# Feed-forward up-projections by Strassen's scheme: seven half-size products, weight sums on GpSimd, six chunks of middle features

## The chip, the cores and the metric

The kernel runs on one core of a Trainium2 chip. The metric is the device time of one launch in microseconds (us). The kernel before was run twice: 2931.71 and 2932.26 us, median 2931.99. The names of the engines are those of the profile: PE is TensorE (matmul), PEld its weight loads, DVE VectorE, ACT ScalarE, POOL GpSimd, SP SyncE, from whose queue most loads are issued.

## What is computed

Two trunk layers over 512 latent tokens and 256 context tokens of width 1024, all in float32. Each layer is a half-step feed-forward, a token mixer, and a second half-step feed-forward, each with its own modulation of shift, scale and gate from a condition vector. The second feed-forward of the last layer needs the latent tokens alone. Cut to what matters here:

```python
D_MODEL, SEQ, CTX_LEN, D_FF, DEPTH = 1024, 512, 256, 2816, 2

def swiglu(h, w_in, w_out):
    g, u = jnp.split(h @ w_in, 2, axis=-1)
    return (jax.nn.silu(g) * u) @ w_out

def half_ffn(x, m, name):
    sh, sc, g = m
    h = modulate(rms_norm(x, prm[name + "_norm"]), sh, sc)
    return x + 0.5 * g * swiglu(h, prm[name + "_w_in"], prm[name + "_w_out"])

xl = half_ffn(xl, mod_l[0:3], "ffn1")
xc = half_ffn(xc, mod_c[0:3], "ffn1")
...
ol, oc = mixer(hl, hc, prm, ctx_out, ropes)
xl = xl + mod_l[5] * ol
xl = half_ffn(xl, mod_l[6:9], "ffn2")
if ctx_out:
    xc = xc + mod_c[5] * oc
    xc = half_ffn(xc, mod_c[6:9], "ffn2")
```

## The kernel before, in words

Activations lie transposed: eight row tiles of 128 features by 768 tokens (512 latent, then 256 context). Float32 operands are split in two parts, a high part rounded to the format that PE multiplies quickly and a low part, the rest; a product of two split operands is three matmuls (high by high, high by low, low by high), written as `three` in `ffn`. Weights are split on the way: `unit` (L206) takes a raw block of 128 x 1024 that SP has loaded (`raw`, L201), ACT casts the high part (L210), and DVE subtracts for the low part (L211). There are two buffers for raw blocks and three sets of high and low parts.

`ffn` (L450) is called four times. The weight matrix of the up-projection comes in 44 units, in turn a gate unit and an up unit of 128 middle features. `product(u)` (L477) runs 8 row tiles x 3 terms x 2 token segments, 48 matmuls, into one of three pairs of PSUM banks: 512 and 258 columns, where 2 columns carry the shift; in the last feed-forward 256 and 258. `gate` (L510) multiplies both results by the token's rms factor (the norm is applied after the product), takes silu with the shift as bias on ACT, multiplies on DVE and splits the outcome. After each chunk of middle features (`CHUNKS`, 8, 7 and 7 tiles) `back` (L527) runs the down-projection of the chunk for each of 8 row tiles, and DVE adds it, times the modulation's gate, to the row tile (L538). After the last chunk `after` prepares the next stage: the sum of squares (`sq_acc`, L411: ACT squares, POOL adds) and the operand of the next feed-forward (`prep`, L422: POOL casts, DVE subtracts). Ahead of a mixer the last chunk is done in two parts, latent tokens first (`D0`, `split`), so that norm and mixer input start under the context's matmuls.

Beside it, `bg` (L385) advances the modulation of later stages by one step of `mod_dve` (L323): it loads 512 KB of weights and runs four multiply-adds of 512 columns on DVE (L338, L340); after four steps come two small groups of matmuls (L358, L367). It is called once per unit and once per row tile of a down-projection. 16 parts of 8 steps are done in this way.

The first feed-forward starts while x is still loading: `late` brings x into its operand within the first products, and the shift's columns follow as matmuls of their own (`shifts`, L502).

Which instruction comes when on an engine is set at build time by a scheduler: it takes what is ready in its own forecast of the run, in the order of the program. On the chip each engine then keeps that order, and waits on semaphores. SBUF beyond the weights is cut into twenty areas A0 to E3 (L153), which each tile takes over from the one before: x in A or D, operands in B and C, the split middle features in D or A (high) and E (low).

## Time and profile before

| what | value |
| --- | --- |
| runs | 2931.71 and 2932.26 us, median 2931.99 |
| span of the profiled execution, first to last instruction | 2929.3 us |
| its instructions | 41724 |
| matmuls, weight loads | 17276, 17276 |
| raw weight loads for each up-projection | 44 of 512 KB |
| loads of modulation weights | 140 of 512 KB |
| mean granted clock of PE | 0.982 |

The span is that of the one execution that was profiled; the median lies 2.7 us above it. A row of busy time by stage gives the stage's bounds and length in us, then for PE, weight loads, DVE, ACT and POOL the busy time with the number of instructions, and at the end the granted clock of PE, the share of the DMA engines' time and GB/s. A row of the timeline gives start, length, engine, line of the kernel, operation, what is written and read, its shape, and how many instructions were merged; in brackets stands idle time before it and what ended it. A row of the chain of waits gives start, length, and what the end of the program was waiting for at that time.

### The profile page before, as it was taken

Reading aid. Unit: us, or ns where it says so; the run is one execution under the profiler, and the core shown is the slowest. Engines: PE = TensorE matmul, PEld = TensorE weight load, DVE = VectorE, ACT = ScalarE, POOL = GpSimd, SP = SyncE. Lnnn points to the kernel's source line nnn. Section 1 sums busy time; section 2 is a strip of 40 time slices with the busy share of each in tenths; the row PEclk is TensorE's granted clock in tenths of the full one; section 3 lists DMA queues with packets and bytes.
Section 4 is the critical chain, followed back from the end, with each engine's and each line's share of the span. In section 5 each row is a group of like instructions: output and inputs, shape, how many; then the busy total and the mean of one; then the engine's idle time right before and its main releaser. Section 6 shows DMA issues by size and latency. Waiting matters only on the chain.

```text
span 2929.3 us, 41724 instructions
## 1 busy us (share of the span) xinstructions
PE 2812.6 (96%) x17276; PEld 2436.2 (83%) x17276; DVE 1708.6 (58%) x2709; ACT 855.1 (29%) x1281; POOL 460.0 (16%) x435
## 2 busy tenths in 40 slices
PE   8999999998479899999999999999999999999999
PEld 5888888887467788888888888888888888898998
DVE  2665666688987676656545533333336779643443
ACT  3211212242156522112122221121224257332221
POOL 1000000035943330000000300000011256300000
PEclk9999999999789999999999999999999999999999
DMA  6433343431010223333433111112124200222232
GB/s 219 129 122 124 120 139 116 127 124 46 31 42 2 72 87 120 118 116 116 140 126 102 59 63 66 59 60 69 59 86 126 65 12 30 87 94 94 88 97 90
DMA packets 93740, 266.62 MB, mean 91 GB/s; under 512 B 8816, under 2 KB 9968, under 8 KB 93552
## 3 DMA queue, kind: packets, MB, share of 16 engines
q1 hardware_dynamic: 86512, 247.89, 26.6%
q10 hardware_dynamic: 5376, 10.83, 1.2%
q0 software_dynamic: 1664, 5.24, 0.5%
q8 instruction: 136, 2.23, 0.3%
q14 instruction: 52, 0.43, 0.0%
HBM read 255.80 MB, written 7.34 MB: 90 GB/s over the span
## 4 chain that ended last, share of the span: by engine, by line
PE 88%; DVE 7%; ACT 2%; issue 1%; DMA 1%; POOL 1%; ACTq 0%; SPq 0%; DVEq 0%; POOLq 0%
PE pa L190 53%; PE pb L190 26%; DVE D L774 3%; PE p L706 2%; PE pb L659 2%; DVE wl L211 1%; PE pa L1035 1%; PE pa L1263 1%; PE p L358 1%; ACT t L661 1%; PE p L193 0%; DMA r<-in_modw 0%; DVE sm L672 0%; PE p L279 0%; DVE C L199 0%
## 5 line engine op out<-in xcount | busy, mean ns | idle before, releaser
L210 ACT CAST wh<-r 128x1024 fp32r<-128x1024 f32 (+3 forms) x334 | 340.6, 1020 | 1517.8 <-PE pa L190 776.1
L190 PE MATMUL pa<-B,wh 128*128 128x512 f32 (+1 forms) x1984 | 492.8, 330 | 10.9 <-DVE D L199 8.6
L190 PE MATMUL pa<-B,wl 128*128 128x512 f32 (+1 forms) x1984 | 487.5, 327 | 0.0
L190 PE MATMUL pa<-C,wh 128*128 128x512 f32 (+1 forms) x1984 | 487.0, 327 | 0.3 <-DVE C L428 0.3
L211 DVE TENSOR_TENSOR wl<-r,wh 128x1024 fp32r<-128x1024 f32 (+3 forms) x334 | 410.7, 1230 | 39.8 <-ACT wh L210 31.0
L190 PEld LDWEIGHTS pa<-B,wh 128*128 128x128 f32 x1984 | 308.6, 190 | 50.9 <-issue 15.8
L190 PEld LDWEIGHTS pa<-C,wh 128*128 128x128 f32 x1984 | 307.9, 190 | 35.7 <-issue 0.7
L190 PEld LDWEIGHTS pa<-B,wl 128*128 128x128 f32 x1984 | 307.7, 190 | 34.1 <-issue 0.5
L199 DVE SCALAR_TENSOR_TENSOR t<-m,sT,t 128x512 f32<-128x512 f32 x392 | 275.7, 752 | 3.9 <-DMA m<-in_modw 2.8
L190 PE MATMUL pa<-E,wh 128*128 128x512 f32 (+1 forms) x919 | 257.7, 347 | 1.3 <-POOL E L215 1.3
L517 DVE COPY sm<-pa 128x2 f32<-128x2 f32 x116 | 18.4, 159 | 395.7 <-PE pa L190 395.1
L190 PE MATMUL pb<-B,wh 128*128 128x512 f32 (+1 forms) x960 | 236.5, 328 | 0.0
L190 PE MATMUL pb<-B,wl 128*128 128x512 f32 (+1 forms) x960 | 234.0, 325 | 0.0
L190 PE MATMUL pb<-C,wh 128*128 128x512 f32 (+1 forms) x960 | 233.5, 324 | 0.0
L190 PE MATMUL pa<-D,wh 128*128 128x512 f32 (+1 forms) x777 | 204.4, 339 | 0.1
L190 PE MATMUL pa<-D,wl 128*128 128x256 f32 (+1 forms) x737 | 196.3, 339 | 0.0
L1416 POOL DMA_DIRECT2D xs<-A x24 | 13.5, 562 | 1089.0 <-DVE A L199 1087.3
L190 PEld LDWEIGHTS pa<-E,wh 128*128 128x128 f32 x919 | 148.2, 188 | 24.3 <-POOL E L215 1.7
L190 PEld LDWEIGHTS pb<-B,wh 128*128 128x128 f32 x960 | 148.6, 189 | 19.6 <-issue 4.2
L190 PEld LDWEIGHTS pb<-C,wh 128*128 128x128 f32 x960 | 148.2, 189 | 16.2
L190 PEld LDWEIGHTS pb<-B,wl 128*128 128x128 f32 x960 | 148.2, 189 | 15.8
L199 DVE SCALAR_TENSOR_TENSOR A<-pa,hg,A 128x256 f32<-128x256 f32 (+1 forms) x95 | 54.9, 614 | 172.1 <-PE pa L190 172.0
(329 smaller groups left out, 4470.3 us busy)
## 6 DMA issues: line engine op xcount, KB each, us to landing
m<-in_modw SPq DMA_DIRECT2D x140, 512.0 KB, 3.7
r<-in_win0a SPq DMA_DIRECT2D x44, 512.0 KB, 4.2
r<-in_win0b SPq DMA_DIRECT2D x44, 512.0 KB, 3.5
r<-in_win1a SPq DMA_DIRECT2D x44, 512.0 KB, 3.4
r<-in_win1b SPq DMA_DIRECT2D x44, 512.0 KB, 3.4
r<-in_wodd SPq DMA_DIRECT2D x18, 512.0 KB, 3.7
r<-in_wout0a SPq DMA_DIRECT2D x20, 448.0 KB, 3.5
r<-in_wout1a SPq DMA_DIRECT2D x20, 448.0 KB, 3.4
```

What stands on the lines that cost most here:

```text
L190: self.nc.tensor.matmul(out, l.bitcast(F32R), r.bitcast(F32R), start=st, stop=sp)
L199: self.nc.vector.scalar_tensor_tensor(o, a, s, b, op0=op0, op1=op1)
L210: pin(self.nc.scalar.copy(hi, r))
L211: pin(self.nc.vector.tensor_tensor(lo, r, hi.bitcast(F32), op=ALU.subtract))
L358: nc.tensor.matmul(p[g:g + 32, :], self.ones[:, 0:32], acc[v][:, q * 256:(q + 1) * 256], start=True, stop=True, tile_position=(0, g))
L517: nc.vector.tensor_copy(w2[:, o:o + 2], p[:, so:so + 2])
L659: pin(nc.tensor.transpose(pt[:, ks], P[:, ks], self.col("ident")))
L661: pin(nc.scalar.copy(PT[:, :m], pt[:, :m]))
L706: self.pin(self.nc.tensor.matmul(self.po[i * 64:(i + 1) * 64, col:col + 128], v, self.PTs[i][:, kt * 128:(kt + 1) * 128], start=(kt == 0), ...
L774: pin(nc.vector.scalar_tensor_tensor(cv, yw, dw[:, w:w + 1], cv, op0=ALU.mult, op1=ALU.add))
L1035: self.pin(nc.tensor.matmul(s[:, o:o + b - a], q[:, ts].bitcast(F32R), k[:, a:b].bitcast(F32R), start=j == 0, stop=j == 2))
L1263: self.pin(nc.tensor.matmul(s[:, a:b], q.bitcast(F32R), k[:, a:b].bitcast(F32R), start=j == 0, stop=j == 1))
```

## The change

The up-projection's product is cut in two along each of its three dimensions: the 1024 features in two halves of 4 row tiles, the output in gate and up, the tokens in two halves (each 256 latent and 128 context tokens, with 2 columns for the shift: 386; 258 in the last feed-forward). Eight half-size products become seven, by sums ahead of them and behind them.

- Weight sums: `group(j)` loads the gate unit R0 and the up unit R1. POOL forms S = R1a + R1b, R0a - R1a, S - R0a, and R0b less the last, each 128 x 512, in place; ACT and DVE split what results, seven blocks of 512 columns (3584), into four sets (`piece`).
- Token sums: seven operand blocks, b11, t1, t2, b21, t3, b22 and t4, take the place of the two operand rows. `xprep` modulates both halves on ACT, forms differences on DVE, and splits (ACT casts, DVE subtracts). `xtail` does b22 and t4 after a mixer's output projection. `xshift` fills the shift's columns.
- Output sums: products 1, 3, 5 and 7 accumulate in one PSUM bank, and ACT copies the bank out in between; products 2 and 6 share a second bank, product 4 has a bank of its own. DVE adds and applies the rms factor, POOL adds once.
- The first two groups of the first feed-forward stay in the old form (`NSTD`), and its down-projections are summed plain over chunks, in the rows of x, which is loaded a second time at the end (`accx`).
- `CHUNKS` becomes 2, 4, 4, 4, 4, 4; a weight unit of the down-projection holds four or two row tiles, 22 units for 24. `bg` is called once per group, and for 6 of 8 row tiles. `D0` goes from 4 to 2. There are three raw buffers for two, and the mask sums of the odd mixer take buffers from these.

```diff
-CHUNKS = (8, 7, 7)
+CHUNKS = (2, 4, 4, 4, 4, 4)
+NSTD = 2
...
-D0 = 4
+D0 = 2
...
-        self.wr = pool("wr", 2)
+        self.wr = pool("wr", 3)
...
-        self.tmq = pool("tmq", 3)
+        self.sp = pool("sp", 1)
...
+    def wt(self):
+        return [self.ws.tile([128, 1024], F32R, name=self.nm(n), tag=n) for n in ("wh", "wl")]
+
+    def piece(self, t, a, b, src):
+        self.nc.scalar.copy(t[0][:, a:b], src)
+        self.nc.vector.tensor_tensor(t[1][:, a:b], src, t[0][:, a:b].bitcast(F32), op=ALU.subtract)
...
+    def xprep(self, d, defer=False):
+        k = d % 4
+        a1, a2 = self.xmod(k)
+        if d < 4:
+            self.xput("b11", k, a1)
+            self.tt(a2, a2, a1, ALU.subtract)
+            self.xput("t1", k, a2)
+            return
+        b1, b2 = self.xmod(d)
+        self.tt(a2, b2, a2, ALU.subtract)
+        self.tt(a1, a2, a1, ALU.add)
+        self.xput("t2", k, a1)
+        self.xput("b21", k, b1)
+        self.xput("t3", k, a2)
+        if not defer:
+            self.xput("b22", k, b2)
+            self.tt(b1, b1, a1, ALU.subtract)
+            self.xput("t4", k, b1)
...
+        self.slots = NF + 6 * len(CHUNKS) - 2
...
+        def group(j):
+            R0, R1 = (self.raw(win[2 * j + i], 1024) for i in range(2))
+            S = self.sp.tile([128, 512], F32, name=self.nm("S"), tag="S")
+            ge = nc.gpsimd
+            ta = self.wt()
+            self.piece(ta, 0, 512, R0[:, 0:512])
+            self.tt(S, R1[:, 0:512], R1[:, 512:1024], ALU.add, ge)
+            self.piece(ta, 512, 1024, S)
+            self.tt(R1[:, 0:512], R0[:, 0:512], R1[:, 0:512], ALU.subtract, ge)
+            self.tt(R0[:, 0:512], S, R0[:, 0:512], ALU.subtract, ge)
+            tb = self.wt()
+            self.piece(tb, 0, 1024, R0)
+            tc = self.wt()
+            self.piece(tc, 0, 1024, R1)
+            self.tt(R0[:, 512:1024], R0[:, 512:1024], R0[:, 0:512], ALU.subtract, ge)
+            td = self.wt()
+            self.piece(td, 0, 512, R0[:, 512:1024])
+            p = self.pd()
+            x, z, y = p[:, 0:W], p[:, 512:512 + W], self.p1()[:, 0:W]
...
+            prod(x, ta, 0, "b11", True)
+            nc.scalar.copy(g1, x)
+            prod(z, ta, 512, "t1", True)
+            nc.scalar.copy(u1, z)
+            prod(x, tb, 0, "t2", False)
+            nc.scalar.copy(g2, x)
+            prod(y, tb, 512, "b21", True)
+            self.tt(g1, y, g1, ALU.add)
+            prod(x, tc, 0, "t3", False)
+            nc.scalar.copy(u2, x)
+            self.tt(u2, u2, u1, ALU.add, ge)
+            prod(z, td, 0, "b22", False)
+            self.tt(g2, z, g2, ALU.add)
+            prod(x, tc, 512, "t4", False)
+            self.tt(G, G, self.rb[:, :2 * W], ALU.mult)
+            self.tt(u1, x, self.rb[:, :W], ALU.mult)
+            self.tt(u2, u2, self.rb[:, W:2 * W], ALU.mult)
+            return G, U
...
+            if d % per == 0 and d // per not in wu:
+                o = off + (d // per) * 128 * 1024
+                wu[d // per] = self.unit(wout[o:o + 128 * 1024].rearrange("(p q) -> p q", p=128), 1024)
...
+            if accx is not None and ci < len(CHUNKS) - 1:
+                if ci == 0:
+                    nc.scalar.copy(self.xv[d], p[:, :nt])
+                else:
+                    self.tt(self.xv[d], p[:, :nt], self.xv[d], ALU.add)
+                return
...
+                if late and j < NSTD:
+                    while u < max(2 * j + 2, n_late):
+                        product(u)
+                        u += 1
+                    if j == 0:
+                        shifts()
+                    late[3](j)
+                    G, U = whole(j)
+                else:
+                    self.bg()
+                    G, U = group(j)
+                gate(G, U, hh[i], hl[i])
...
+            if last and accx is not None:
+                xr = self.rows("D", NT)
+                for d in range(8):
+                    nc.scalar.dma_start(xr[d], accx[:, d, :])
...
-                if not (last and d > 5):
+                if d % 4 != 3 and not (last and d > 5):
                     self.bg()
...
-                tm = self.tmq.tile([128, 256], F32, name=self.nm("tm"), tag="tm")
+                tm = self.wr.tile([128, 1024], F32, name=self.nm("r"), tag="r")[:, :256]
```

More of the change, by code (lines that the diff above doesn't have):

```diff
@@ L448, in shift_cols, with xblocks, xblock @@
         self.split(xs[:, :, 0, :], xs[:, :, 1, :], self.mod[L][:, m * 8:(m + 1) * 8, :], "dve")
-    def ffn(self, win, wout, lat_only, after, mid=None, late=None, fill=(), raws=(), split=None):
+    def xblocks(self, tags, lat_only):
+        self.w = 256 if lat_only else 384
+        self.xtags = list(tags)
+        self.X, self.Xv = {}, {}
+    def xblock(self, *names):
+        W = self.w + 2
+        for n in names:
+            ts = [self.area(self.xtags.pop(0))[:, :4 * W] for _ in range(2)]
+            self.Xv[n] = [t.rearrange("p (k n) -> p k n", k=4) for t in ts]
+            self.X[n] = [[t[:, k * W:(k + 1) * W] for k in range(4)] for t in ts]
@@ L540, in ffn @@
+            for a, b, v in segs:
+                o, g = self.xv[d][:, a:b], self.hg[:, d, v:v + 1]
+                if accx is not None:
+                    self.tt(o, p[:, a:b], o, ALU.add)
+                    self.stt(o, o, g, xr[d][:, a:b], ALU.mult, ALU.add)
+                else:
+                    self.stt(o, p[:, a:b], g, o, ALU.mult, ALU.add)
         n_late = NLATE if late else 0
+        rbq = rb[:1] + [None] * RBW + rb[1:] if late else [[], [], rb[:1], rb[1:2], [], rb[2:]]
         u = j = 0
@@ L1433, in ready @@
             def ready():
+                if L == 0:
+                    gate(2)
                 self.need(L, 4)
```

260 lines of the change are left out of this document (162 added, 98 removed).

## The prediction

> **What bounds the kernel now.** I read the page's busy shares and its chain first, then busy time by stage (the four feed-forwards are stages 1, 4, 5 and 7), then the chain of waits in order of time, then the timeline inside a feed-forward. All rows are of the profiled execution of before.
>
> ```profile
> span 2929.3 us, 41724 instructions
> PE 2812.6 (96%) x17276; PEld 2436.2 (83%) x17276; DVE 1708.6 (58%) x2709; ACT 855.1 (29%) x1281; POOL 460.0 (16%) x435
> ...
> PE 88%; DVE 7%; ACT 2%; issue 1%; DMA 1%; POOL 1%; ACTq 0%; SPq 0%; DVEq 0%; POOLq 0%
> ```
>
> ```profile
> 62.00:604.00 542.00, 541.93 (x3124) 467.58 (x3125) 355.18 (x575) 115.17 (x141) 13.63 (x16) 0.99 0.40 124
> 604.00:1018.00 414.00, 332.27 (x2179) 282.73 (x2178) 334.93 (x505) 191.37 (x371) 212.35 (x160) 0.90 0.16 48
> 1018.00:1104.00 86.00, 85.05 (x487) 74.03 (x487) 58.36 (x70) 22.70 (x27) 30.50 (x21) 1.00 0.28 88
> 1104.00:1640.00 536.00, 534.51 (x3076) 458.39 (x3075) 314.70 (x494) 109.45 (x130) 19.84 (x16) 1.00 0.36 116
> 1640.00:2220.00 580.00, 576.72 (x3271) 503.04 (x3270) 218.69 (x308) 134.67 (x167) 31.30 (x28) 1.00 0.22 71
> 2220.00:2550.00 330.00, 318.72 (x2225) 268.26 (x2224) 248.47 (x495) 162.23 (x300) 136.92 (x184) 0.99 0.18 54
> 2550.00:2929.00 379.00, 375.52 (x2631) 351.64 (x2629) 161.79 (x228) 98.29 (x113) 1.54 (x2) 1.00 0.28 92
> ```
>
> The columns after the stage's length are PE, PEld, DVE, ACT and POOL busy, then granted clock and DMA. In the feed-forwards PE idles 0.07 of 542, 1.5 of 536, 3.3 of 580 and 3.5 of 379 us at full clock. DVE is at 40 to 65%, POOL almost unused. So these stages, some 2037 us, are PE time and nothing else, and a matmul removed there is time removed, as long as nothing new is late.
>
> **What PE saves.** The chain shows a pair of weight units and, for the last feed-forward (512 tokens), the same, and a down-projection of 512 columns:
>
> ```profile
> 1688.95 16.96 PE pa L190 x96
> 2572.44 11.55 PE pa L190 x96
> 2776.66 9.72 PE pa L190 x42
> ```
>
> The first is 176.7 ns a matmul at 385 columns in the mean (512 and 258), the second 120.3 ns at 257 (256 and 258): 0.44 ns a column and 7 ns on top. The line gives 232.7 ns at 512, and the third row has 231.4, so it holds over the whole span of sizes. A matmul of 386 columns is then 177.1 ns, one of 258 is 120.8. Each matmul has its own weight load before and after the change, and at 120.3 ns a load and its matmul still keep up, so loads do not become the limit.
>
> Seven products of 4 row tiles and 3 terms are 84 matmuls where there were 96. A group (gate and up of 128 features) goes from 16.96 to 84 x 0.1771 = 14.88 us, in the last feed-forward from 11.55 to 84 x 0.1208 = 10.15. The first feed-forward keeps two groups in the old form (NSTD), so 20 + 22 + 22 groups save 2.08 us each, 133.1 us, and 22 save 1.40, 30.8 us. Together **163.9 us**. Down-projections keep their matmuls; six chunks only cut them otherwise.
>
> **What a group asks of the other engines.** Rows from the timeline with POOL quiet; the second figure is the length of the piece, x2 or x4 its instructions, and starts that follow each other give a step:
>
> ```profile
> 1120.03 2.73 DVE L199 SCALAR_TENSOR_TENSOR t<-m,sT,t 128x512 f32<-128x512 f32 x4
> 1123.85 0.95 DVE L196 TENSOR_TENSOR t<-pb,rb 128x768 f32<-128x768 f32 x1
> 1124.71 1.22 DVE L211 TENSOR_TENSOR wl<-r,wh 128x1024 fp32r<-128x1024 f32 x1
> 1125.85 1.14 DVE L199 SCALAR_TENSOR_TENSOR t<-t,sm,t 128x512 f32<-128x512 f32 x2
> ```
>
> ACT and POOL:
>
> ```profile
> 1123.46 1.05 ACT L210 CAST wh<-r 128x1024 fp32r<-128x1024 f32 x1 [5.91 <-PE pb L190]
> 1127.02 0.84 ACT L227 CAST D<-t 128x768 fp32r<-128x768 f32 x1 [2.51 <-DVE t L199]
> 1133.28 1.12 ACT L523 ACTIVATE t<-t,sm 128x512 f32<-128x512 f32 x2 [0.33 <-DVE t L196]
> ```
>
> ```profile
> 580.83 2.40 POOL L196 TENSOR_TENSOR acc<-acc,t 128x512 f32<-128x512 f32 x2
> ```
>
> ```profile
> L220 ACT CAST B<-p 128x384 fp32r<-128x384 f32 x4 | 1.9, 480 | 10.0 <-PE p L1202 10.0
> ```
>
> DVE's starts are 0.86 us apart after 768 columns and 1.14 after 1024, 1.12 ns a column. Per group: weight pieces 3584 columns (2048 before), three reads of PSUM of 386, the rms factor over 772 and 386, gate 768, low part 772: 7440 columns, **8.3 us**; in the last feed-forward 6160, 6.9 us. A background step of the modulation adds 2.73: one per group now instead of two, 55 in each of the first two feed-forwards, and the rest of the 128 (16 parts of 8) moves into the third, where DVE has room. POOL: four sums of 512 at 1.20 and one of 386 at about 0.9 (by columns), **5.7 us**; last feed-forward 5.4. ACT: casts 3.8, four copies out of PSUM at 0.48, silu 1.12, cast 0.84: 7.7 of 14.88. Each of the three engines alone fits under PE.
>
> DVE and POOL together are the question. The convolution shows both at work (first DVE alone and beside POOL, seven instructions each; then POOL's cycle beside DVE and alone):
>
> ```profile
> 680.41 7.45 DVE L774 SCALAR_TENSOR_TENSOR D<-D,small,D 128x783 f32<-128x783 f32 x7
> 703.11 13.34 DVE L774 SCALAR_TENSOR_TENSOR D<-D,small,D 128x783 f32<-128x783 f32 x7
> ```
>
> ```profile
> 714.10 1.53 POOL L771 TENSOR_SCALAR A<-D,small 128x783 f32<-128x783 f32 x1
> 715.71 2.17 POOL L772 TENSOR_TENSOR D<-D,A 128x783 f32<-128x783 f32 x1
> 717.98 1.52 POOL L771 TENSOR_SCALAR A<-D,small 128x783 f32<-128x783 f32 x1
> ...
> 802.98 0.93 POOL L771 TENSOR_SCALAR A<-D,small 128x783 f32<-128x783 f32 x1
> 804.00 1.57 POOL L772 TENSOR_TENSOR D<-D,A 128x783 f32<-128x783 f32 x1
> 805.66 1.52 POOL L771 TENSOR_SCALAR A<-D,small 128x783 f32<-128x783 f32 x1
> ```
>
> In 13.34 us DVE did what takes 7.45 alone, and POOL 13.34/3.88 = 3.44 cycles, which alone take 2.68 each, 9.2. So 16.7 us of work took 13.3: the two all but queue for each other, at 0.80 of the sum. For a group the sum is 8.3 + 5.7 = 14.0, with a background step 16.7, in the last feed-forward 12.3; at 0.80 it is 11.2, 13.4 and 9.8, against PE's 14.88, 14.88 and 10.15. PE stays the bound, closely in the last.
> The Trainium skill's page "SBUF — State Buffer" (Who interferes with whom) states that the port pair which GpSimd and VectorE share is an exclusive lock: of a VectorE instruction with two SBUF inputs and a GpSimd one that reads SBUF, the second fully blocks. The convolution agrees in kind (1.06 to 1.91 us an instruction), in size only to 0.80; with full blocking groups would take 16.7 and 12.3 us, which is the second rival below.
>
> **What comes late.** PE waits in order, so DVE's delay reaches it where a matmul needs a DVE result. Before shows one such wait, with POOL at work:
>
> ```profile
> 1622.42 2.92 DVE L199 SCALAR_TENSOR_TENSOR C<-A,am,B 128x512 fp32r<-128x512 f32 x2
> 1625.26 0.41 DVE L360 COPY t<-p 64x256 f32<-64x256 f32 x1
> 1625.72 0.60 PE L193 MATMUL p<-small,t 64*128 64x2 f32 x4 [1.49 <-DVE t L360]
> ```
>
> 1. Modulation matmuls: about 28 half-modules in the first two feed-forwards, 0 to 1.5 us each; I take half, 21 us, for by the stage row DVE has some slack.
> 2. New in the group: three products reuse the bank x, so products 3, 5 and 7 wait for ACT's copy, with one product (2.13 us; 1.45 in the last) in between. A cast of 1.05 in front and the copy of 0.48 still fit. Behind them on ACT stand silu and the cast of u, which wait for DVE. 0 to 2.73 us a group (one background step of DVE in front); nearer to nothing, since the copy comes first in time: 0.2 a group in 64, 13 us, and 0.6 in the last feed-forward with its smaller margin, 13 us.
> 3. Six chunks: before a down-projection the last gate must end: two factors 0.86, gate 1.07, cast 0.84, low part 0.86, some 3.9 us with handovers, behind 3 x 6 matmuls, 3.2 us (before 6 or 7 x 6, 6.4 or more); after the chunk of two behind 1.1 us. Over all chunks 0 to 21 us, as PE can or cannot start another row tile meanwhile: 14. Evictions double in number (8 a chunk); 1.07 us each under 24 matmuls, 4.2 us.
> 4. First feed-forward: blocks in areas B and C can be written only when product u = 3 has read them: 16 casts of 0.48 and 20 DVE steps of 0.43, some 9 us, behind chunk 0's down-projections (96 matmuls, 17 us) and three products. 0 to 12: 6. The reload of x (8 DMAs on ACT's queue) lands as below in 7.1 us, under four products and a row tile, 12.7.
> 5. Layer 0's end: for row tiles 4 to 7 DVE has 1.07 + 0.57 + 8 x 0.43 = 5.1 us (7.8 with a step) per 4.24 of PE; late by 3 to 14, less two products that need only tiles 0 to 3 (4.25), plus the last chain: 0 to 12, I take 8.
> 6. Handoff to both mixers: a row tile's context part falls from 21 to 12 matmuls, 2.5 to 1.4 us, under which POOL's sum of squares (3.38/2 below) no longer fits; 0 to 10 each, 4 taken: 8.
>
> ```profile
> A<-in_xT SPq DMA_DIRECT2D x8, 384.0 KB, 7.1
> ```
>
> ```profile
> 2205.58 2.48 PE pb L190 x21
> ```
>
> ```profile
> 2225.15 3.38 POOL L196 TENSOR_TENSOR acc<-acc,t 128x256 f32<-128x256 f32 x2 [13.19 <-ACT t L418]
> ```
>
> Weights take no wait: the SP queue issues the same two 512 KB loads per group, a third buffer is added, and the sets free up two products ahead. The odd mixer's mask sums take raw buffers from the same pool now; only its first output units load beside them, and its PE idles 11 of 330 us as it is: 0.
>
> **Sum.** 21 + 26 + 14 + 6 + 8 + 8 = 83 us of waits. Span 2929.3 - 163.9 + 83 = 2848.4; the median of the runs, 2931.99, lies 2.7 over the span, so **2851 us**, 2.8% faster; this case's own range 2815 to 2890. With items 3 to 6 as they are, the time is that of before at (163.9 - 36)/86 = 1.49 us of wait a group.
>
> **Rivals.**
> - PE alone sets the end, as in the stages of before: all waits together 15 us. For it: each engine alone has room, and the list of work lets PE go on with other tiles. Against it: DVE and POOL near their joint limit. 2932 - 164 + 15 = 2783.
> - DVE and POOL in full turn: 42 groups at 16.7 (1.8 over PE) and 22 at 12.3 (2.15 over), 77 + 47 = 124, with items 3 to 6 160: 2928, no change. For it: both mixers, where the sum of the two is over the stage (1.17 and 1.32 by the rows above), have PE idle 3 and 20%. Against it: 0.80. This is also what the skill's rule would give.
> - Slower: ACT's copy out of bank x stands behind the cast of u, which waits for DVE with a step or the weight pieces in front, 2.73 us in every group. 86 x 2.73 = 235, with 36: 2932 - 164 + 271 = 3039. It decides from 1.49 on. For it: ACT goes in order and PE cannot pass the wait. Against it: in before ACT's order follows PE's events closely.
> - That PE's time does not follow columns is excluded by the fit; even by count 84 to 96 is the same ratio.
>
> **How the numbers follow.** Forecast 0.44, PE alone 0.18, full turn 0.25, slower 0.13. A measurement tells about 2%, that is below 2873 or over 2991. Faster: 0.18 and some four fifths of 0.44: 0.54. Slower: most of 0.13: 0.12. The rest, 0.34, within 2%. Range 2780 to 2975: it takes in the middle of the first rival and all of the second; about 0.07 lies below and 0.13 above.
>
> **What would show it.** PE: 5376 matmuls of 386 columns near 177 ns and 1848 of 258 near 121; instructions down by 1032 to about 16244, busy time by about 164. POOL up by some 480 us. A group in the chain 14.9 to 15.6 us, in the last feed-forward 10.2 to 10.8. Sums of 512 on POOL over 1.2 us, DVE's pieces over 1.22. Wrong if groups take 16.5 us or more, if PE's idle time names ACT's copies by more than 1 us a group, or if more than 60 us go to the seams between chunks and stages.

## The result and the profile after

The changed kernel takes 3090.75 us (3088.81 and 3092.69), the kernel before 2931.99: 1.0542 times as long, interval [1.0511, 1.0572]. The forecast was 2851, its range 2780 to 2975; the time lies 240 us above the forecast and outside the range, on the slower side, which had 0.12.

The page of the changed kernel, span and busy times, to be read beside the two lines of before:

```profile
span 3086.9 us, 41874 instructions
PE 2784.1 (90%) x16244; PEld 2430.2 (79%) x16244; DVE 2211.6 (72%) x3341; ACT 1236.0 (40%) x2083; POOL 985.8 (32%) x825
```

PE has 1032 instructions fewer, as predicted, and POOL 526 us more (480 forecast). But PE's busy time falls by 28.5 us, not by 164, and its idle time grows from 116.7 to 302.8 us. -28.5 + 186.1 is the 157.6 us by which the span is longer.

The four feed-forwards by the windows (after the length: PE, PEld, DVE, ACT, POOL busy with counts, granted clock, DMA share, GB/s):

```profile
62.00:642.00 580.00, 536.21 (x2884) 474.77 (x2884) 457.02 (x667) 209.88 (x330) 147.71 (x110) 0.96 0.35 110
1112.00:1685.00 573.00, 529.82 (x2850) 471.38 (x2851) 446.13 (x655) 191.27 (x298) 148.85 (x105) 0.97 0.35 109
1743.00:2300.00 557.00, 538.36 (x2870) 480.82 (x2870) 330.46 (x453) 191.40 (x294) 148.78 (x118) 0.99 0.25 82
2651.00:3087.00 436.00, 378.66 (x2374) 331.51 (x2374) 263.34 (x360) 169.25 (x277) 135.36 (x107) 0.98 0.25 81
```

Where PE idled 0.07, 1.5, 3.3 and 3.5 us before, it idles 44, 43, 19 and 57 us, and in all four the clock is below full. In the last, DVE is busy for 263 and POOL for 135 of 436 us; from the trace, at least one of the two is at work in 335 us, and neither in 101. So neither alone nor both together are full, and still PE waits. That points to lateness, not to an engine's rate; the experiments below test it.

PE's waits in the order of their size, those that the kernel before does not have in this size:

```profile
engine line waited for: us in total, times, longest us
PE pa L194 <- DVE t L200: 33.9, 34, 2.9
...
PE p L281 <- POOL acc L200: 23.8, 4, 17.2
...
PE pa L194 <- ACT t L647: 17.9, 26, 1.6
PE pa L194 <- ACT wh L214: 17.4, 13, 6.7
PE pb L194 <- DVE t L200: 16.4, 12, 3.8
PE pa L194 <- ACT wh L223: 13.7, 25, 0.6
PE pb L194 <- ACT t L647: 13.2, 18, 1.7
...
PE pa L194 <- ACT t L645: 8.2, 4, 6.0
```

L647 is ACT's copy of z, L200 on `t` in a group is DVE's addition that reads z. None of z's readers was among the prediction's waits, which named only the copies out of x. Both halves of what happens show in one group of the second feed-forward; the rows of all engines, in order of time, PE's with the idle time ahead of them and its releaser in brackets:

```profile
1303.16 1.41 DVE L203 SCALAR_TENSOR_TENSOR t<-m,sT,t 128x512 f32<-128x512 f32 x2
...
1304.80 0.47 ACT L647 COPY t<-pa 128x386 f32<-128x386 f32 x1
...
1305.32 0.62 PE L194 MATMUL pa<-C,wh 128*128 128x386 f32 x2
...
1311.19 1.63 POOL L200 TENSOR_TENSOR r<-S,r 128x512 f32<-128x512 f32 x1
1311.58 3.06 DVE L203 SCALAR_TENSOR_TENSOR t<-m,sT,t 128x512 f32<-128x512 f32 x2
...
1312.77 1.32 POOL L200 TENSOR_TENSOR t<-t 128x386 f32<-128x386 f32 x1
...
1316.36 0.55 DVE L200 TENSOR_TENSOR t<-pa,t 128x386 f32<-128x386 f32 x1
...
1316.96 0.93 PE L194 MATMUL pa<-D,wh 128*128 128x386 f32 x2 [2.11 <-DVE t L200]
```

First, product 3 adds to x. It starts at 1305.32, 0.05 us after ACT has ended its copy of z (1304.80 + 0.47), the product of just before. x and z are the two halves of one PSUM tile, p, and a product into one half starts only when the reader of the other half is done. In the same way product 2 (into z) follows the copy out of x behind product 1, product 6 (into z) the copy out of x behind product 5, and product 7 (into x) the addition out of z behind product 6. The whole trace shows it: in the median of the 86 groups the next matmul into the tile starts 0.05 us behind each of these four readers. Product 5, which has product 4 ahead of it in the program, starts 0.13 us behind the copy that follows product 3: in the group shown, the build has put 10 of the 12 matmuls of product 4 into earlier gaps. Second, DVE is late for that addition: its two multiply-adds of the modulation take 1.41 us at 1303.16, when POOL is quiet, and 3.06 at 1311.58, when POOL makes two sums. Product 7 then starts after 2.11 us of idle, and its first pair of matmuls takes 0.93 us where the pair at 1305.32 took 0.62. The windows around it tell why; the clock stands behind the busy times:

```profile
1296.00:1316.00 20.00, 18.85 (x110) 17.00 (x108) 16.99 (x25) 5.69 (x9) 5.98 (x4) 1.00 0.35 107
1316.00:1322.00 6.00, 5.04 (x20) 5.04 (x21) 5.69 (x7) 1.98 (x3) 1.94 (x1) 0.72 0.25 84
```

After the wait of 2.11 us the granted clock is 0.72 in the mean of 6 us, that is, at half for 0.28 x 2 x 6 = 3.4 of them.

From the starts of all matmuls in the trace one can add up the gaps: by how much each start in the new products lies later after the matmul before it than that one takes undisturbed (177 ns for 386 columns, 121 for 258). The columns: gaps over 0.5 us; of the smaller ones, those at half clock; and at full clock those of 0.15 to 0.5 us and of 0.05 to 0.15 us. The second and third row are runs of the next section.

| us beyond the undisturbed rate (gaps) | > 0.5 | 0.15 to 0.5 | 0.05 to 0.15 | half clock |
|---|---|---|---|---|
| changed kernel | 130.7 (122) | 24.7 (84) | 50.6 (505) | 19.7 |
| x in its own tile (e1_own) | 124.5 (76) | 11.9 (52) | 16.4 (156) | 17.3 |
| and no weight sums (e8_own_nosums) | 26.9 (8) | 5.9 (25) | 5.5 (57) | 9.7 |

So 226 us are lost with the new products, and 505 of the gaps are some 0.1 us long: the hand-back of the tile even when its reader is on time, like the one at 1305.32, too short to be counted as idle. The median start to start at full clock is 177 and 120 ns.

### The profile page after: what moved, and what is told of

It reads as the page before. It is cut to its first block, busy times and chain, and to the rows that moved or that the text cites. A ratio compares the mean times of both kernels' runs of the same rounds, so it can differ in the third digit from the quotient of the medians.

```text
span 3086.9 us, 41874 instructions
## 1 busy us (share of the span) xinstructions
PE 2784.1 (90%) x16244; PEld 2430.2 (79%) x16244; DVE 2211.6 (72%) x3341; ACT 1236.0 (40%) x2083; POOL 985.8 (32%) x825
## 5 line engine op out<-in xcount | busy, mean ns | idle before, releaser
L223 ACT CAST wh<-r 128x512 fp32r<-128x512 f32 (+1 forms) x344 | 286.9, 834 | 693.0 <-PE pa L194 424.3
L194 PE MATMUL pa<-E,wh 128*128 128x512 f32 (+1 forms) x1732 | 421.0, 352 | 22.5 <-ACT wh L214 17.2
L224 DVE TENSOR_TENSOR wl<-r,wh 128x512 fp32r<-128x512 f32 (+1 forms) x344 | 350.6, 1020 | 99.2 <-ACT wh L223 93.1
L200 POOL TENSOR_TENSOR S<-r 128x512 f32<-128x512 f32 x86 | 122.9, 1429 | 685.5 <-DMA r<-in_win0a 191.4
L194 PEld LDWEIGHTS pa<-E,wh 128*128 128x128 f32 x1732 | 282.5, 191 | 73.6 <-ACT wh L214 20.3
L194 PE MATMUL pa<-B,wh 128*128 128x386 f32 (+2 forms) x968 | 248.9, 340 | 30.5 <-ACT wh L223 11.3
L214 ACT CAST wh<-r 128x1024 fp32r<-128x1024 f32 (+2 forms) x146 | 150.7, 1034 | 285.3 <-PE pa L194 170.4
L194 PE MATMUL pa<-E,wl 128*128 128x512 f32 (+1 forms) x866 | 248.0, 349 | 3.0 <-DVE wl L215 3.0
L200 POOL TENSOR_TENSOR r<-r 128x512 f32<-128x512 f32 x86 | 121.4, 1411 | 399.1 <-DVE wl L224 394.7
L194 PE MATMUL pb<-E,wh 128*128 128x512 f32 (+1 forms) x892 | 218.2, 351 | 7.2 <-DVE t L200 5.6
L215 DVE TENSOR_TENSOR wl<-r,wh 128x1024 fp32r<-128x1024 f32 (+2 forms) x146 | 189.8, 1302 | 47.3 <-ACT wh L214 46.6
L200 DVE TENSOR_TENSOR t<-t,rb 128x386 f32<-128x386 f32 (+3 forms) x172 | 123.6, 719 | 139.5 <-POOL t L200 137.2
L194 PE MATMUL pa<-D,wh 128*128 128x386 f32 (+2 forms) x768 | 205.7, 353 | 13.9 <-DVE t L200 10.9
L194 PE MATMUL pa<-C,wh 128*128 128x386 f32 (+2 forms) x736 | 191.5, 344 | 28.3 <-ACT t L647 16.0
L194 PEld LDWEIGHTS pa<-B,wh 128*128 128x128 f32 x968 | 166.7, 194 | 55.3 <-ACT wh L223 19.2
L200 POOL TENSOR_TENSOR r<-S,r 128x512 f32<-128x512 f32 x86 | 140.3, 1631 | 207.9 <-DVE wl L224 122.3
L194 PE MATMUL pa<-B,wl 128*128 128x386 f32 (+3 forms) x556 | 173.1, 333 | 5.1 <-DVE wl L224 5.1
L194 PEld LDWEIGHTS pb<-E,wh 128*128 128x128 f32 x892 | 146.5, 191 | 31.2 <-issue 4.3
L194 PEld LDWEIGHTS pa<-C,wh 128*128 128x128 f32 x736 | 125.5, 193 | 51.2 <-ACT t L647 27.6
L194 PEld LDWEIGHTS pa<-D,wh 128*128 128x128 f32 x768 | 134.2, 191 | 36.2 <-DVE t L200 17.0
```

What stands on the lines that cost most here:

```text
L194: self.nc.tensor.matmul(out, l.bitcast(F32R), r.bitcast(F32R), start=st, stop=sp, skip_group_check=add)
L200: (e or self.nc.vector).tensor_tensor(o, a, b, op=op)
L214: pin(self.nc.scalar.copy(hi, r))
L215: pin(self.nc.vector.tensor_tensor(lo, r, hi.bitcast(F32), op=ALU.subtract))
L223: self.nc.scalar.copy(t[0][:, a:b], src)
L224: self.nc.vector.tensor_tensor(t[1][:, a:b], src, t[0][:, a:b].bitcast(F32), op=ALU.subtract)
```

## The experiments

Each time is a median of runs that shared their chip with the kernel before, given as a ratio to it with its interval. Stage times below are taken between the first norm products of the feed-forwards (the matmuls that add up POOL's squares) in the profiled executions. A changed program also gets another order of instructions from the build, so the worth of an edit includes what its new order does.

**x in a PSUM tile of its own.**

```
-            x, z, y = p[:, 0:W], p[:, 512:512 + W], self.p1()[:, 0:W]
+            y, z, x = p[:, 0:W], p[:, 512:512 + W], self.p1()[:, 0:W]
```

> The changed kernel, with one line edited: x, the accumulator that is copied out three times, lies in a PSUM tile of its own, and z and y share the two-bank tile. The computation is that of the changed kernel. Theory A (the order treats the two halves of a two-bank PSUM tile as one, so a product into one half waits for the reader of the other half, which stands right behind the product just before it; there is no product in between): the waits named under the groups, 34 + 16 us for DVE and 18 + 13 us for ACT, mostly go, and with them much of the 128 us at half clock that they bring; 3090 less 80 to 150 us, 2940 to 3010, clock mean 0.97 or more. Theory B (DVE and POOL are the bound, by their joint load, whatever the tiles): less than 30 us come back, 3060 or more. Theory C (the seams between chunks and stages take it): less than 20 us, 3070 or more.

Measured: 2990.3 us, 1.0197 [1.018, 1.0214]. 100 us come back for one line that leaves each engine the same number of instructions: theory A. The slack that the prediction counted on is now there: the next matmul into x's tile starts 1.4 us, in the median, behind the copies that follow products 3 and 5, where into the shared tile it was 0.13 and 0.05. The clock's mean went from 0.962 to 0.966, less than I expected, since other waits remain. Their list has a new head:

```profile
PE p L194 <- ACT t L645: 56.8, 31, 11.7
```

L645 is the copy behind product 1. ACT's own order shows why, in a group of the last feed-forward:

```profile
2717.53 0.72 ACT L666 ACTIVATE t<-t 128x512 f32<-128x512 f32 x1 [1.07 <-DVE t L200]
2718.16 1.03 ACT L223 CAST wh<-r 128x1024 fp32r<-128x1024 f32 x1
...
2719.09 0.36 ACT L645 COPY t<-p 128x258 f32<-128x258 f32 x1
...
2719.51 0.51 PE L194 MATMUL p<-C,wh 128*128 128x258 f32 x2 [1.59 <-ACT t L645]
```

The copy stands behind silu of the group before, which waited for DVE, and a cast of weights. This is close to the mechanism of the prediction's slower rival, which had the cast of u in front of the copy.

**No weight sums.** The four sums on POOL are left out and the pieces cut from the raw halves (`self.piece(ta, 512, 1024, R1[:, 0:512])` and the like), with the shared tile and then with x in its own.

> The changed kernel without the four weight sums of a group on POOL: the pieces are cut from the raw halves, so four of the seven products multiply other weights; DVE, ACT and PE do as many instructions as before. Theory A (waits on the other half of the tile, without slack): ACT's part of the waits, 31 us, stays, DVE's part of 50 shrinks since its instructions are no longer stretched; 3090 less 30 to 80 us, 3010 to 3060. Theory B (joint load of DVE and POOL): the stretch is gone and with it nearly all of the loss, 2850 to 2930. Theory C (seams): less than 30 us, over 3060.

> The changed kernel with x in a PSUM tile of its own and without the four weight sums of a group on POOL (pieces cut from the raw halves, four of seven products multiply other weights). Theory B (what is left over PE's own time, some 190 us, is the joint load of DVE and POOL): 2990 less 80 or more, below 2910. Theory A with ACT's order as the rest: the sums stretch DVE, which ACT waits for, so part of it: 2990 less 30 to 60, 2930 to 2960.

Measured: 3011.69 us, 1.0277 [1.026, 1.0295], and with x in its own tile 2855.31 us, 0.9735 [0.9721, 0.975]. So the sums cost 79 us with the shared tile and 135 without; the tile costs 100 with the sums and 156 without; together 235, more than 100 + 79. It looks as if one late hand-back hid another. The first time lies at the edge of what theory A gave, the second is theory B's, below 2910: with the tile mended, the sums are most of the rest. Without the two causes the kernel takes 2855, near the forecast of 2851, but without making the weight sums at all.

**No multiply-adds of the background modulation**, seven of eight on DVE.

> The changed kernel without the multiply-adds of the background modulation on DVE (the first product of each half and the loads stay, seven of eight multiply-adds are left out, so the modulation vectors are other numbers). Theory A (no slack between a product and the reader of the other half): DVE is late less often, ACT's waits stay; 3090 less 30 to 70, 3020 to 3060. Theory B (joint load of DVE and POOL): a background step is 2.7 of some 14 us of load a group in the first two feed-forwards and a third of the third; 3090 less 80 or more, below 3010. Theory C: no change, over 3070.

Measured: 3025.99 us, 1.032 [1.0305, 1.0336]: 65 us less, as theory A had it. So DVE's own work counts too, where it makes DVE late. The last feed-forward did not change (436.2 us for 435.3).

**Six chunks in the kernel before**, then the same with as many background steps as before.

```
-CHUNKS = (8, 7, 7)
+CHUNKS = (2, 4, 4, 4, 4, 4)
```

> The kernel before with its middle features in six chunks (2, 4, 4, 4, 4, 4) in place of (8, 7, 7), nothing else. Theory C (seams): over 60 us more, 2990 or more. The prediction's third item has 14 us (0 to 21) and the doubled evictions; theories A and B expect that or less: 2932 to 2955.

```
-                if not (last and d > 5):
+                if d % 2 == 0 and not (last and d > 5):
```

> The kernel before with six chunks (2, 4, 4, 4, 4, 4), and background steps of the modulation at every other row tile of a chunk, so that a feed-forward makes 67 of them as with (8, 7, 7) (66) and not 90. Theory C (the seams themselves cost, a shorter gate window and twice the evictions): as with six chunks alone, 3030 or more. Theory D (six chunks alone lost its 108 us, 83 of them in the first feed-forward, to the background steps, which came more often and held up the low halves of the weights on DVE; the seams are cheap): 2932 to 2965.

Measured: 3039.37 us, 1.0374 [1.0358, 1.039], then 3004.14, 1.0242 [1.0225, 1.0259]. Of 108 us, 36 went with the background steps that came oftener, and 72 stay with the chunks: 3004 lies between theory C (3030 or more) and theory D (up to 2965). 40 of the 72 lie ahead of the second feed-forward's norm, mostly at the very start, as the first window shows, in the second of these runs and then in the kernel before:

```profile
62.00:162.00 100.00, 80.74 (x404) 67.83 (x404) 74.72 (x128) 18.58 (x27) 0.00 (x0) 0.81 0.45 136
```

```profile
62.00:162.00 100.00, 99.93 (x557) 87.67 (x558) 70.77 (x125) 26.55 (x32) 0.00 (x0) 0.93 0.40 126
```

The clock goes to 0.81. In the run with six chunks and as many background steps, PE's longest waits of the first feed-forward all lie in this window:

```profile
PE p L358 <- DVE t L199: 11.0, 3, 5.6
PE pa L190 <- ACT wh L210: 4.5, 1, 4.5
PE pa L190 <- DVE A L199: 3.3, 1, 3.3
```

The largest is that of the modulation's matmuls for the background multiply-adds on DVE. So even with as many steps as before, part of the 72 us comes from where the steps fall, and not from the seams. The rest is 12 us in the second feed-forward, 16 in the third with its mixer and 6 in the last.

**The gate behind the next group's copies**: silu and cast of a group are pinned on ACT behind the first two copies of the next group; x in its own tile.

```
             prod(z, ta, 512, "t1", True)
             nc.scalar.copy(u1, z)
+            if mate:
+                gate(*mate)
...
-                    G, U = group(j)
-                gate(G, U, hh[i], hl[i])
+                    G, U = group(j, mate)
+                    mate = (G, U, hh[i], hl[i])
```

> The changed kernel with x in a PSUM tile of its own, and the gate of a group (silu and the casts) placed on ACT behind the first two copies out of PSUM of the next group, pinned there; the last group of a chunk is gated at the chunk's end. Computation as in the changed kernel. Theory A (what is left of the waits in the groups, 57 us named on the first copy out of x, is ACT's order: that copy stands behind silu and the cast of the group before, which wait for DVE): 2990 less 40 to 80, 2910 to 2950. Theory B (joint load of DVE and POOL, the order does not matter): 2975 or more.

Measured: 2972.11 us, 1.0136 [1.012, 1.0151]. 18 us: less than the 40 I gave as its least. The wait on that copy fell from 56.8 to 18.8 us, but waits for DVE grew (`PE p L194 <- DVE t L200` from 13.5 to 35.5). ACT's order was one link; with it mended, DVE's lateness shows in its place.

**D0 = 4 again**, with x in its own tile.

> The changed kernel with x in a PSUM tile of its own, and D0 back at 4: the context part of row tiles 4 to 7, not 2 to 7, is made last before a mixer. Theory E (the 23 and 25 us that each mixer's stage lost come from D0 = 2: six short context parts, 1.4 us each, behind which POOL's sums of squares and the second norm run late): 2990 less 25 to 45, 2945 to 2965. Theory B (POOL's work of the feed-forward itself is late at the handoff, whatever D0): 2980 to 2995. It can also lose, since the first parts of the norm then start later: 3000 or more.

Measured: 2989.25 us, 1.0193 [1.0178, 1.0208]; no change. Theory E falls.

**POOL as busy as before, but nothing waits for its sums**: they add a constant tile into an unused one; x in its own tile.

```
-            self.tt(S, R1[:, 0:512], R1[:, 512:1024], ALU.add, ge)
+            self.pin(ge.tensor_tensor(S, c, c, op=ALU.add))
```

> The changed kernel with x in a PSUM tile of its own; POOL makes its four sums of 512 columns in each group as before, but of a constant tile into an unused one, held in place in POOL's order, and the pieces are cut from the raw halves (four of seven products multiply other weights). So POOL is as busy as with the sums, and nothing waits for them. Theory B (contention: POOL's instructions hold up DVE's): as with x alone, 2960 to 2990. Theory F (latency: load, four sums one after the other, cast and low half make a chain longer than a group, and the raw buffers come free late): as without the sums, 2855 to 2885.

Measured: 3017.43 us, 1.0298 [1.0283, 1.0313]: 162 us over the run without sums, and theory F, the length of the chain from load to low half, falls. Theory B holds in kind; the time is 27 us over its range and over the run with real sums, and the fixed order on POOL may be why, which no run tests. The two runs differ in POOL's sums, on which no other engine waits, and in that u2 + u1 stands behind them in POOL's order; DVE waits for that sum as long in both, 99.5 and 98.4 us. The busy times, without sums and with unused ones:

```profile
PE 2676.7 (94%) x16244; PEld 2419.8 (85%) x16244; DVE 2083.3 (73%) x3341; ACT 1237.1 (43%) x2083; POOL 479.0 (17%) x481
```

```profile
PE 2723.1 (90%) x16244; PEld 2433.1 (81%) x16244; DVE 2272.1 (75%) x3341; ACT 1234.2 (41%) x2083; POOL 959.1 (32%) x825
```

With 480 us more on POOL, DVE is busy for 189 us longer with the same 3341 instructions; ACT's do not change. By form (busy, mean ns of one, idle ahead), without sums:

```profile
L200 DVE TENSOR_TENSOR t<-pa,t 128x386 f32<-128x386 f32 x86 | 48.0, 558 | 76.7 <-PE pa L194 74.2
L200 DVE TENSOR_TENSOR t<-t,rb 128x386 f32<-128x386 f32 x64 | 35.8, 560 | 87.7 <-POOL t L200 87.7
```

and with them:

```profile
L200 DVE TENSOR_TENSOR t<-t,rb 128x386 f32<-128x386 f32 x64 | 84.4, 1318 | 86.6 <-POOL t L655 86.6
L200 DVE TENSOR_TENSOR t<-pa,t 128x386 f32<-128x386 f32 x86 | 47.6, 553 | 59.1 <-PE pa L194 59.0
```

The instruction with both inputs in SBUF goes from 560 to 1318 ns; the one that takes an input from PSUM stays at 553. That is what the Trainium skill's page "SBUF — State Buffer" (Who interferes with whom) states: a VectorE instruction with two SBUF inputs contends with a GpSimd one that reads SBUF, and one with at most one SBUF input, outside the two-port modes, does not.

**Buffers and banks.** Four raw weight buffers (paid for with one of eight buffers of pool t); the price alone; and three tiles for x, y and z with the late gate and four raw buffers.

```
-        self.wr = pool("wr", 3)
+        self.wr = pool("wr", 4)
...
-        self.st = pool("st", 8)
+        self.st = pool("st", 5)
...
-        self.tmp = pool("tmp", 8)
+        self.tmp = pool("tmp", 7)
```

> The changed kernel with x in a PSUM tile of its own and four raw weight buffers in place of three (paid for with one of eight buffers of the pool t, and three of eight of the small pool st). Theory F (the chain from load to low half is too long for the buffers): the next group's load starts earlier, 2990 less 40 to 100, 2890 to 2950. Theory B (contention): no change, 2975 to 3000.

> The changed kernel with x in a tile of its own, seven buffers of the pool t in place of eight, and five of eight of st, the price that the run with four raw buffers paid. If the 89 us which that run lost come from the missing buffer of t (groups hold two, the background steps two or three), this one has 3060 or more, and four raw buffers gain nothing; if it has 2990 to 3000, the fourth raw buffer itself did harm.

> The changed kernel with x, y and z each in a tile of its own (x in the three pairs of banks, z and y in the two single banks), the gate of a group behind the first two copies of the next on ACT, and four raw buffers as in the run beside it. Computation as in the changed kernel. Theories A and F together (tile halves, ACT's order, buffers): the gains add, 2972 less 40 to 100, 2870 to 2930. Theory B (contention): no better than 2960.

Measured: 3079.49 us, 1.0506 [1.049, 1.0521]; 3025.32, 1.0321 [1.0305, 1.0336]; 2993.93, 1.0214 [1.0197, 1.0231]. Seven buffers of t (and five of st) cost 35 us and the fourth raw buffer 54 more, where it should have helped: neither of the two outcomes I had written down. The third run pays the same price, so it does not show what separate tiles are worth. That a fourth raw buffer is no remedy is shown. Why it does harm is not, but the traces show what changes: in 24 of the 86 groups three weight sums run on POOL between the copy of u2 and u2 + u1, where with three buffers it is never more than two, and DVE's waits for that sum grow from 127 to 212 us.

**The sums on DVE**: u2 + u1 alone (x in its own tile, late gate); the four weight sums alone (x in its own tile); the same with the shared tile; all of them with both other edits.

```
-            self.tt(u2, u2, u1, ALU.add, ge)
+            self.tt(u2, u2, u1, ALU.add)
...
-            self.tt(S, R1[:, 0:512], R1[:, 512:1024], ALU.add, ge)
+            self.tt(S, R1[:, 0:512], R1[:, 512:1024], ALU.add, gw)
```

(`gw` is `nc.vector`; likewise for the other three weight sums.)

> As the run with x in its own tile and the gate behind the next group's copies (2972 us), and the sum u2 + u1 of a group on DVE in place of POOL. Theory G (DVE, in order, waits for that sum on POOL, 127 us in all and up to 3.4 us at a time, with the weight sums in front of it in POOL's queue): 2972 less 30 to 70, 2900 to 2942. Theory B (what counts is how long POOL's weight sums hold up DVE's instructions): within 15 us, 2957 to 2985, since DVE takes 0.43 to 0.55 us on more.

> The changed kernel with x in a tile of its own and the four weight sums of a group on DVE in place of POOL. Computation as in the changed kernel. DVE has 4 x 0.64 us a group more of its own, 344 x 0.64 = 220 us, and is no longer held up by the sums, 131 us. If DVE's time reaches the end one to one: 2990 + 90 = 3080, range 3040 to 3100. If waiting for POOL's long sums was what cost (latency), 2990 less 20 or more.

> The changed kernel with one edit: the four weight sums of a group on DVE in place of POOL; the two halves of the PSUM tile as they are. Computation as in the changed kernel. If tile and sums are two separate losses (100 and 93 us): 3090 less 93, 2985 to 3010. If the sums cost through the missing slack alone (a late DVE shows because products wait for it at once): more than that comes back with each, below 2980; if DVE is late anyway with the halves as they are: 3020 or more.

> The changed kernel with three edits: x in a PSUM tile of its own, the gate of a group behind the first two copies of the next on ACT, and all sums of a group (four of weights, u2 + u1) on DVE. Computation as in the changed kernel. If the steps measured by themselves add (2898 with the first and the weight sums, 18 us for the gate, 22 us for u2 + u1): 2858, range 2845 to 2885, faster than both kernels. If DVE is now full (79% busy with the weight sums alone): 2890 or more.

Measured: u2 2950.41 us, 1.0064 [1.0049, 1.0079], 22 less, between the two theories; weight sums 2897.53, 0.9884 [0.9869, 0.9899], 93 less; with the shared tile 3025.95, 1.0323 [1.0309, 1.0337], 65 less, the third outcome: products that hand the tile back at once wait for DVE anyway; all 2880.18, 0.9824 [0.981, 0.9837], in the range given but 22 over its middle.

The second is the surprise. I expected 90 us more, as DVE gets 243 us of sums of its own, four rows like the first below; on POOL, in the run with x in its own tile, the same sum is the second:

```profile
L200 DVE TENSOR_TENSOR r<-r,r 128x512 f32<-128x512 f32 x86 | 59.5, 692 | 1.5
```

```profile
L200 POOL TENSOR_TENSOR r<-r,r 128x512 f32<-128x512 f32 x86 | 121.0, 1407 | 6.7
```

DVE's busy time rises by 73 us (2214.1 to 2287.3) and the kernel is 93 us faster. A sum on DVE takes a known place in its order; a sum on POOL lengthens whatever DVE happens to run beside it, and nothing in the order allows for that. That this is why the same work costs less on the busier engine fits all the runs; it is argued, and no run takes the order apart. Against the run with neither (2855), the four sums cost 42 us on DVE and 135 on POOL. The fastest kernel here that computes the layers is the last, 1.8% under the kernel before:

```profile
span 2870.9 us, 41463 instructions
PE 2678.7 (93%) x16244; PEld 2418.3 (84%) x16244; DVE 2316.0 (81%) x3771; ACT 1233.3 (43%) x2083; POOL 408.3 (14%) x395
```

```profile
1640.00:2220.00 580.00, 572.92 (x3210) 533.23 (x3210) 414.01 (x659) 222.11 (x351) 21.89 (x27) 0.99 0.28 90
2510.00:2870.00 360.00, 345.93 (x2328) 315.36 (x2326) 280.50 (x433) 158.05 (x258) 0.00 (x0) 1.00 0.28 96
```

PE is busy for 99% in the third feed-forward and 96% in the last, where the changed kernel had 97 and 87.

**Seven products in the third feed-forward only**, with x in its own tile and the late gate, the others as in the kernel before with chunks of 8, 7 and 7.

> A kernel of both: the first, second and fourth feed-forward as in the kernel before (eight products, chunks of 8, 7 and 7), the third alone by seven products in six chunks, with x in a PSUM tile of its own and the gate behind the next group's copies. Computation as in both kernels. The third had 892 us with its mixer in the kernel before and 870 with these two edits; the others go back to their times of before, less what the third's background steps and its last operand blocks, made at its start, cost: 2905 to 2925, faster than both. If the seams eat it: 2930 to 2945.

Measured: 2903.69 us, 0.9908 [0.9891, 0.9924], 1 us under the range expected. It is 0.9% under the kernel before, less than the version above.

## Why the prediction was wrong, point by point

| us | first FFN and mixer | second FFN | third FFN and mixer | last FFN | sum |
|---|---|---|---|---|---|
| before | 1077.2 | 584.6 | 892.1 | 375.4 | 2929.3 |
| less PE's saving, by the prediction | 1035.6 | 538.8 | 846.3 | 344.6 | 2765.3 |
| changed | 1112.0 | 630.7 | 908.8 | 435.3 | 3086.8 |
| x in its own tile | 1090.9 | 603.0 | 877.4 | 419.3 | 2990.6 |
| and no weight sums | 1057.0 | 573.2 | 865.1 | 358.3 | 2853.6 |
| own tile, late gate, sums on DVE | 1060.2 | 573.2 | 865.9 | 371.6 | 2870.9 |

- **PE's saving (163.9 us): right.** Undisturbed matmuls start every 177 and 120 ns, against 177.1 and 120.8. The rate per column held; it is what PE does between them that went wrong.
- **Item 2, the waits inside a group (26 us): the step that failed.** The text says: "products 3, 5 and 7 wait for ACT's copy, with one product (2.13 us; 1.45 in the last) in between". There is no product in between. x shares its tile with z, and products 2, 3, 6 and 7 each wait for a reader that starts only when the product just before them has ended; for product 7 that reader is DVE, not ACT. I had followed the variable x and not the tile that it is cut from, though the line that cuts both halves out of p was before me. Slack was taken for some 2 us and was zero: the gaps in the new products come to 226 us against the 26. The build's order puts matmuls of y or of the next group into the gap, but only as many as the copy takes when it is on time. One line put right is worth 100 us, 156 with the weight sums away.
- **DVE and POOL ("at 0.80 it is 11.2, 13.4 and 9.8 ... PE stays the bound, closely in the last"): right as a rate, wrong as a test.** In the last feed-forward of the changed kernel at least one of the two is at work in 335 of 436 us, so their joint rate was no limit; and still, with x in its own tile, the sums cost 61 us there (419.3 to 358.3). What counted was whether the tile's readers, DVE above all, were in time for each hand-back, and beside POOL single DVE instructions take twice as long. I had put the stretch into the throughput and not into the wait of item 2. That the two engines hold each other up was in the prediction, and its consequence drawn only for the rate. With x in its own tile the sums cost 135 us where nothing was set aside for them beyond item 2. (The rows read as POOL alone, at 802.98, have DVE at work beside them; at 0.93 and 1.57 us they are among the shortest of their kind all the same, so the 0.80 is hardly touched.)
- **The clock after a wait: not costed.** The mean granted clock is 0.962 for 0.982: (1 - 0.962) x 3086.9 = 117 us of full-speed time that the clock withheld, 53 before. Not all of it is lost, since PE also waits in these stretches; between the new products' matmuls it costs 20 us by the table above.
- **The remaining items: right in sum, partly by luck.** Without the two causes 2853.6 - 2765.3 = 88 us are left against 83 forecast, item 2 included. By place: 21 us ahead of the second feed-forward, 34 in it, 19 in the third with its mixer, 14 in the last. Within the list sizes were off both ways: in the changed kernel PE's waits on POOL's squares at the handoffs are 24 us against 8 (12.5 without the two causes), and the modulation's matmuls (item 1) wait 8 us against 21. "Weights take no wait" failed too: PE waits 50 us for the casts and low halves of weights (L214, L223, L215, L224), 19 without the two causes, and none by name in the kernel before.
- **Item 3, seams (14 us).** In the kernel before the six chunks cost 72 us, with 11 us of waits for background steps among them, so this item was too small; in the new form the chunks cannot be taken apart from the rest, and the whole remainder is 88. I had read the first feed-forward as one stage, and not its first 100 us by themselves, where DVE is at 71% in the kernel before.
- **The rivals.** "Full turn" named DVE and POOL, by their rate, and had 2928; POOL's sums were 79 to 135 us of the 240, but by lateness and not by rate. The slower rival came nearest in time, 3039. A copy held up on ACT behind work that waits for DVE is real (56.8 us once x has its own tile), but mending it is worth 18 us, and it stood in the second row behind the shared tile. Its break-even of 1.49 us a group held: the loss over the forecast is 240/86 = 2.8 us a group beyond the 0.3 counted, and the kernel is slower.
- **What would show it.** Groups of 16.5 us or more was the sign that came: from copy of z to copy of z, inside a chunk, it is 16.7 us in the median of the first three feed-forwards, 14.3 in the last (15.0 and 10.1 without the two causes). The test for ACT's copies, over 1 us a group, missed: they are 48 us by name (0.6 a group), and the waits for DVE's L200 50, some 42 of them for the addition that reads z. The loss was spread over two engines, 505 gaps of 0.1 us and the clock.

What stays open: why a fourth raw buffer costs 54 us; how much of the 135 us of the sums falls on which hand-back; how much of each difference is the build's new order; and how the remainder of 88 us divides between the seams, the handoffs to the mixers (on which D0 has no part) and the waits inside the groups.

## What to carry to other kernels

Write beside each product its true releaser: the reader of the whole tile that it writes into, not of the slice, and count the products that lie between; where that count is zero, every delay of the reader's engine is PE's delay. Test a helper engine by the latency that it adds to instructions on that path and not by the sum of busy times: here work moved to a "free" engine that slows the one on the path cost 135 us, and 42 on the path's own engine. And price a wait of 2 us or more with the half clock behind it.

## What the runs showed of the hardware

- A wait of 2.11 us was followed by some 3.4 us at half the granted clock (0.72 in the mean of the 6 us from 1316). In the changed kernel's trace, 7 of 8 waits of 2 to 3 us that began at full clock were followed by such a stretch, and 6 of 131 waits of 0.5 to 1.5 us. The Trainium skill's page "TensorE: Matmul & The Clock Gate" (Part 1: The HAM clock gate) states half rate after an idle window of about 3.4 us that runs free of the program; the length of the slow stretch agrees, but here a wait of 2.11 us brought it on, well under that length.
- POOL's sums of 512 columns take 1.40 to 1.61 us beside DVE, 0.69 to 0.75 on DVE itself; beside POOL, DVE's product of two SBUF operands of 386 columns takes 1318 ns for 560, and one with a PSUM operand 553 for 558.
- 505 us of sums on POOL stretched DVE by 131 us (2083.3 to 2214.1) and the kernel by 135: nearly one to one, with DVE at 74%. With 480 us of unused sums it was 189 us for DVE and 162 for the kernel.
